# A short-sequence attention kernel: the output stores of 34 of 48 units on GpSimd's queue instead of 24, ten of them directly behind its last load

## Chip, cores, metric

One core of a Trainium2 chip. The time is the device time of one execution in microseconds (us), as a median of several executions. A "span" is the time from the first to the last instruction of a profiled execution, about 1.8 us less than that execution's time. Executions of this kernel scatter by about 1% on either side, so small differences are judged by the means of fast runs of the same rounds and their 95% intervals. A run is called slow when it lies more than 1.5% above the fastest of the same kernel, and fast otherwise. In profile lines POOL is GpSimd, SP is SyncE, ACT is ScalarE, DVE is VectorE and PE is TensorE; a q marks the sequencer of an engine, which issues its DMAs.

## The reference

```python
batch, n_heads, seq, head_dim = 32, 12, 128, 64        # q, k, v: f32
scores = (1.0 / np.sqrt(64)) * np.matmul(q, k.transpose(0, 1, 3, 2))
attn = np.exp(scores - scores.max(-1, keepdims=True))
attn = attn / (attn.sum(-1, keepdims=True) + 1e-8)
return np.matmul(attn, v)
```

There are 384 heads. The kernel works on **units** of 8 heads (48 units). q and k are loaded in 12 pieces of 4 units each, v in 12 groups of 4 units.

## The kernel before

GpSimd issues all loads (they cast f32 to bf16) and, among them, the stores of the first 24 units. SyncE issues the other 24, and not before unit `HELD` = 40 is normalised, so that its stores do not compete with the last loads. A store of two units goes out as two DMAs of 256 KB, so each unit costs one such DMA; I call that "a store" below.

```python
    stores = [1, 1] + [2] * ((NU - 4) // 2) + [1, 1]        # units per output buffer
    NQ, NVB, NVE, NP, NT, NA = 4, 2, 8, 4, 2, 4             # v: two buffers
    LAG, MIXED, HELD = 14, 24, NU - 8
    # ... one output buffer for each entry of stores, none is used twice
    mixed = [c for c in range(len(stores)) if sum(stores[:c + 1]) <= MIXED]

    def store(c):
        name = "POOL" if c in mixed else "SP"
        # ... emits one or two dma_start on that engine
        last = first + n - 1
        op(name, ("store", c), emit, [("N", last if c in mixed else max(last, HELD))])

    def act_keep(m):                                        # ScalarE: v out of PSUM
        # ... also waits for the landing of the v group that m + 1 begins
        op("ACT", ("K", m), lambda: keep_v(m), deps, ["act_pe"], v_landing(m + 1))

    # loads sorted by the step that needs them; a v load waits until the buffer
    # of two groups earlier is read
    todo = list(range(len(stores)))
    for _, kind, x in loads:
        pool_load(kind, x)
        while kind == "k" and todo[0] in mixed and sum(stores[:todo[0] + 1]) <= 4 * x - LAG:
            store(todo.pop(0))
    for c in todo:
        store(c)
```

The softmax here doesn't subtract the row's maximum and nothing guards it: scores larger than these inputs give would overflow.

## Time and profile before

| | before |
|---|---|
| time, median (3 runs) | 138.57 us |
| span of the profiled run | 135.7 us |
| busiest engine | TensorE, 70% |
| DMA moved | 37.75 MB read, 12.58 MB written |
| stores: GpSimd / SyncE | 24 / 24 |
| unit 40 normalised | 114.08 us |
| last unit normalised | 126.25 us |
| last store landed | 134.0 us |

The rows of 40 slices are read like this: each digit (in the GB/s row each number) is one slice of 3.4 us, and the digit is the busy share in tenths. The slices, the waits and the hole are shown in the prediction. Two lines of GpSimd's timeline (start, duration, engine, line, instruction; in brackets the idle time before it and what ended it):

```profile
95.92 0.73 POOL L400 DMA_DIRECT2D k_b<-in_k_dram  x1
103.43 0.74 POOL L388 DMA_DIRECT2D v_b<-in_v_dram  x1 [6.78 <-PE v_ps L187]
```

The second is GpSimd's last instruction in the kernel before: it has nothing to do for the last 32 us. "Landed" in this text is the time at which the sixteenth of a DMA's sixteen completion records came (one from each DMA engine); the first of them shows how far the quick DMA engines are. (The two DMAs of a store of two units count on one semaphore, so there only the first record of the first and the last of the second are sure.)

### The profile page before, as it was taken

The numbers are of one execution on the slowest core, as the hardware profiler recorded it, in microseconds if no ns is written. First come the engines' busy times: TensorE is split into PE (matmuls) and PEld (weight loads), VectorE is DVE, ScalarE is ACT, GpSimd is POOL, SyncE is SP. The second block draws the span as 40 slices with busy tenths as digits, with TensorE's granted clock in tenths as the row PEclk, the third lists the DMA queues.
The fourth block names the chain that finished last, engine by engine and source line by source line (L and its number), as shares of the span: only waits on it lengthen the run. The fifth ranks groups of instructions, "written<-read, shape, count | busy, mean of one in ns | idle before, by whom it ended". The sixth has DMA issues, their size and how long they took to land. (4 is left out here: it accounts for less than half of the span.)

```text
span 135.7 us, 6988 instructions
## 1 busy us (share of the span) xinstructions
PE 94.8 (70%) x3072; PEld 67.4 (50%) x3072; DVE 89.6 (66%) x204; ACT 73.8 (54%) x97; POOL 44.0 (32%) x65
## 2 busy tenths in 40 slices
PE   0055789899999786777499788599787979864000
PEld 0043367676667554555376556466555666542000
DVE  1155457999999699299079499288598798655200
ACT  0002548787885871862664754754855867793000
POOL 6920006064392935805900942801402000000000
PEclk9999999999999999999959999959999999999555
DMA  2999999999999999999999999999999960999993
GB/s 16 176 197 210 209 215 208 204 213 205 213 279 214 212 355 205 208 354 204 210 345 223 215 345 220 218 341 224 218 276 212 207 100 21 341 338 342 342 339 132
DMA packets 21320, 31.56 MB, mean 233 GB/s; under 512 B 1344, under 2 KB 13632, under 8 KB 21312
## 3 DMA queue, kind: packets, MB, share of 16 engines
q0 software_dynamic: 14784, 25.17, 89.9%
q1 hardware_dynamic: 6528, 6.29, 14.0%
q8 instruction: 4, 0.07, 0.2%
q14 instruction: 4, 0.03, 0.1%
HBM read 37.75 MB, written 12.58 MB: 371 GB/s over the span
## 5 line engine op out<-in xcount | busy, mean ns | idle before, releaser
L238 ACT ACTIVATE attnT<-s_ps 128x1024 bf16<-128x1024 f32 x48 | 49.4, 1030 | 0.3 <-PE s_ps L213 0.2
L233 ACT CAST v_e<-v_ps 128x512 bf16<-128x512 f32 x48 | 28.2, 588 | 36.6 <-PE v_ps L187 20.3
L173 PE MATMUL qk_ps<-ident,pair 128*128 128x128 bf16 x384 | 32.1, 231 | 15.2 <-PEq L466 14.9
L187 PE MATMUL v_ps<-v_b,sel 128*32 128x256 bf16 x768 | 31.5, 287 | 10.8 <-PEq L466 10.8
L256 DVE COPY qkT<-qk_ps 128x1024 bf16<-128x1024 bf16 x48 | 32.8, 683 | 5.7 <-PE qk_ps L173 4.6
L268 DVE TENSOR_TENSOR o_sb<-o_ps,recip 128x512 f32<-128x512 f32 x48 | 33.2, 691 | 1.7
L173 PEld LDWEIGHTS qk_ps<-ident,pair 128*128 128x128 bf16 x384 | 23.9, 103 | 19.7 <-issue 18.3
L388 POOL DMA_DIRECT2D v_b<-in_v_dram x12 | 9.2, 771 | 58.9 <-PE v_ps L187 54.3
L187 PEld LDWEIGHTS v_ps<-v_b,sel 128*32 128x32 bf16 x768 | 16.8, 98 | 17.2 <-issue 13.1
L225 PE MATMUL o_ps<-v_e,attnT 128*32 128x65 bf16 x1536 | 21.2, 197 | 3.9 <-PEq L466 3.5
L247 DVE COPY pair<-q_b 128x1024 bf16<-128x1024 bf16 x24 | 10.5, 437 | 19.1 <-DMA q_b<-in_q_dram 18.9
L225 PEld LDWEIGHTS o_ps<-v_e,attnT 128*32 128x32 bf16 x1536 | 15.7, 98 | 9.8 <-issue 6.3
L213 PE MATMUL s_ps<-qkT 64*128 64x128 bf16 x384 | 19.5, 222 | 0.6 <-PEq L466 0.5
L213 PEld LDWEIGHTS s_ps<-qkT 64*128 64x128 bf16 x384 | 11.1, 95 | 11.0 <-issue 11.0
L377 POOL DMA_DIRECT2D out_dram<-o_sb x22 | 15.9, 747 | 0.0
L265 DVE RECIPROCAL recip<-o_ps 128x8 f32<-128x8 f32 x48 | 9.7, 203 | 7.4 <-PE o_ps L225 6.6
L247 DVE COPY pair<-k_b 128x1024 bf16<-128x1024 bf16 x24 | 10.2, 426 | 0.0
L400 POOL DMA_DIRECT2D q_b<-in_q_dram x12 | 8.8, 732 | 1.0 <-SPq L93 1.0
L400 POOL DMA_DIRECT2D k_b<-in_k_dram x12 | 8.8, 735 | 0.0
L233 ACT ACT_TABLE_LOAD x1 | 1.3, 1283 | 12.8 <-DMA v_b<-in_v_dram 12.8
L545 DVE COPY sel<-ident 128x128 bf16<-128x128 bf16 x2 | 0.4, 223 | 1.7 <-POOL ident L520 1.7
L374 POOL DMA_DIRECT2D out_dram<-o_sb x2 | 1.5, 753 | 0.0
(8 smaller groups left out, 1.4 us busy)
## 6 DMA issues: line engine op xcount, KB each, us to landing
q_b<-in_q_dram POOLq DMA_DIRECT2D x12, 512.0 KB, 12.1
k_b<-in_k_dram POOLq DMA_DIRECT2D x12, 512.0 KB, 13.9
v_b<-in_v_dram POOLq DMA_DIRECT2D x12, 512.0 KB, 10.2
out_dram<-o_sb POOLq DMA_DIRECT2D x24, 256.0 KB, 14.4
out_dram<-o_sb SPq DMA_DIRECT2D x24, 256.0 KB, 3.3
```

The lines of the kernel that those rows point to most:

```text
L173: i = nc.tensor.transpose(p[:, :, r4, jj, :], x[:, r].rearrange("p a d -> p (a d)"), ident[:])
L187: x = nc.tensor.matmul(t[r4 * 32:(r4 + 1) * 32, i, :, :], lhsT=pick[:, w * nh + i, jv, :], rhs=v_b[g % NVB][:, :n, (4 * jv + r4) * D:(4 * ...
L213: i = nc.tensor.matmul(t[:, a, h, :], lhsT=x[p, 1, 4 * w + h, :], rhs=x[p, 0, 4 * w + h, :], start=True, stop=True)
L225: y = nc.tensor.matmul(t[h * SO:(h + 1) * SO, a, r * (D + 1):(r + 1) * (D + 1)], lhsT=x[:, a, h, r * SO:(r + 1) * SO], rhs=v_e[m % NVE][:, ...
L233: return nc.scalar.copy(v_e[m % NVE][:, :, :D], v_ps[:].rearrange("p (n e) -> p n e", e=D))
L238: return nc.scalar.activation(out=attnT[u % NA][:].rearrange("p a h (r s j) -> p (a h r) s j", r=4, j=J), in_=s_ps[u % 2][:].rearrange("p ...
L247: return nc.vector.tensor_copy(pair[t_index[t] % NP][:], src[:, 8 * b:8 * b + 8])
L256: return nc.vector.tensor_copy(x.rearrange("p h (r j s) -> p (h r) j s", r=4, j=J)[:, :, 2 * b:2 * b + 2, :].rearrange("p x j s -> p x (j ...
L265: nc.vector.reciprocal(r[:], o4[:, :, :, D]).then_inc(s_r, 1)
L268: return nc.vector.tensor_mul(o[:, :, w, :].rearrange("p a (r d) -> p a r d", d=D), o4[:, :, :, :D], r[:].unsqueeze(3).to_broadcast([128, ...
L377: e.dma_start(out=dst[:, a], in_=src[:, a]).then_inc(s_o[lane(c)], 16)
L400: nc.gpsimd.dma_start(out=bufs[x % NQ][:], in_=rows[R][:, n:n + 2, :]).then_inc(sm[x % NQ], 16)
```

## The change

The intent is to give the DMA engines something to do between the last load and unit 40: ten units' stores are queued on GpSimd directly behind its last load. The 24 stores among the loads are also spread more evenly, which puts them later.

```diff
-    LAG, MIXED, HELD = 14, 24, NU - 8
+    MIXED, OWN, HELD = 24, 34, NU - 8
-    mixed = [c for c in range(len(stores)) if sum(stores[:c + 1]) <= MIXED]
+    own = [c for c in range(len(stores)) if sum(stores[:c + 1]) <= OWN]
-        return c % 4 + (4 if c in mixed else 0)
+        return c % 4 + (4 if c in own else 0)
-        name = "POOL" if c in mixed else "SP"
+        name = "POOL" if c in own else "SP"
-        op(name, ("store", c), emit, [("N", last if c in mixed else max(last, HELD))])
+        op(name, ("store", c), emit, [("N", last if c in own else max(last, HELD))])
-        while kind == "k" and todo[0] in mixed and sum(stores[:todo[0] + 1]) <= 4 * x - LAG:
+        while kind == "k" and sum(stores[:todo[0] + 1]) <= MIXED * (x - 4) / (len(supers) - 5):
             store(todo.pop(0))
```

## The prediction

> **What bounds the kernel now.** I read the page's slices first, then its queues, then the sync engine's waits, and then narrow windows round the one hole in the slices.
>
> The page's rows of 40 slices (3.4 us each), its queues and its DMA issues:
> ```profile
> DMA  2999999999999999999999999999999960999993
> GB/s 16 176 197 210 209 215 208 204 213 205 213 279 214 212 355 205 208 354 204 210 345 223 215 345 220 218 341 224 218 276 212 207 100 21 341 338 342 342 339 132
> ...
> q0 software_dynamic: 14784, 25.17, 89.9%
> q1 hardware_dynamic: 6528, 6.29, 14.0%
> ...
> out_dram<-o_sb POOLq DMA_DIRECT2D x24, 256.0 KB, 14.4
> out_dram<-o_sb SPq DMA_DIRECT2D x24, 256.0 KB, 3.3
> ```
> The DMA engines are full from the second slice on, except for one hole two slices wide, some 20 us before the end. No compute engine is above 70%. So the time is roughly the DMA work, plus the start, plus the hole, plus the end. Before the hole GpSimd's queue runs (loads and 24 units' stores), after it SyncE's (the other 24 units' stores, 341 GB/s). GB/s counts written bytes; loads are cast from f32 to bf16, so 210 GB/s of loads is about 420 read.
>
> Why SyncE starts late (waits of SP), and the hole in half microseconds (the two last columns are the DMA share and GB/s):
> ```profile
> SPq L377 <- DVEq L477: 113.3, 1, 113.3
> ...
> 108.50:109.00 0.50, 0.11 (x12) 0.05 (x2) 0.50 (x2) 0.50 (x1) 0.00 (x0) 1.00 1.20 201
> ...
> 109.50:110.00 0.50, 0.50 (x18) 0.34 (x16) 0.50 (x1) 0.00 (x0) 0.00 (x0) 1.00 0.80 125
> 110.00:110.50 0.50, 0.50 (x28) 0.33 (x24) 0.30 (x2) 0.31 (x1) 0.00 (x0) 1.00 0.46 74
> 110.50:111.00 0.50, 0.33 (x32) 0.20 (x28) 0.50 (x2) 0.50 (x2) 0.00 (x0) 1.00 0.38 63
> 111.00:111.50 0.50, 0.35 (x7) 0.39 (x8) 0.47 (x3) 0.50 (x1) 0.00 (x0) 1.00 0.21 33
> 111.50:112.00 0.50, 0.50 (x17) 0.39 (x18) 0.50 (x1) 0.20 (x1) 0.00 (x0) 1.00 0.00 0
> ...
> 115.00:115.50 0.50, 0.45 (x8) 0.46 (x8) 0.47 (x2) 0.50 (x1) 0.00 (x0) 1.00 0.79 254
> ```
> The last load, v of group 11, ends here: the quick DMA engines finish at 109.5, the slow ones 2 us later. SyncE waits for unit 40's normalisation (13.39 + 0.69 after 100: done at 114.08) and its first bytes move after 115. Against a full share of about 1.12, the stretch 109.5 to 115.1 (5.6 us) did about 0.8 us of work: **4.7 us lost**. Meanwhile the output of units 24 to 39 lay ready, one unit every 2 us.
>
> The end (DVE and SP in the timeline):
> ```profile
> 125.56 0.69 DVE L268 TENSOR_TENSOR o_sb<-o_ps,recip 128x512 f32<-128x512 f32 x1
> 130.02 1.51 SPq L374 DMA_DIRECT2D out_dram<-o_sb  x2
> ```
> The last unit is done at 126.25, but SyncE, working off its 24 stores, issues its last one at 130.8. So today the store queue sets the end, 4.5 us behind the compute. By the trace's completion records that store has landed at 134.0; the span ends at 135.67, 1.67 us later.
>
> **What the Trainium skill says.** (1) "DMA: Bandwidth & Descriptors", section "Issuing engines are not separate DMA queues": all DMAs end on the same 16 engines, and another issuer only saves issue time. The trace agrees, with 342 GB/s of stores in SP's tail at a share above 1, so moving ten stores to GpSimd is worth only what it puts into the hole. (2) Same page, "Queues, rings and completion order": an engine goes round the queues that have work. Two queues in the tail thus share, and neither leaves engines idle; no trace here shows the two side by side. (3) Same page, "SWDGE vs HWDGE vs iDMA": a software-queue packet has up to 4096 B. The counts agree: SyncE's 6528 packets over 24 stores are 272 each (256 of 1 KB, 16 for completion), while q0's 14784 less my count of 12864 for the loads leaves 80 per store (64 of 4 KB and 16). (4) Same page, "Latency and other measured facts": some engines lag on the software path. The trace's lag was 1.1 us early and is 2.2 us from 60 us on (v of group 11: first completion 109.6, sixteenth 111.8).
>
> **The change part by part.** The completion records give each transfer's price. Without stores between, a q, k, v trio lands every 7.55 us (v at 12.7, 20.3, 27.9). With four stores per trio it is 10.0 (v at 75.4 and 85.4), so a GpSimd store between loads costs (10.0 - 7.55) / 4 = **0.62 us**. SyncE's 24 landed from 116.4 to 134.0: 17.6 / 23 = **0.765 us** each.
>
> (a) The 24 stores among the loads. I walked both loops by hand. Units stored ahead of v of group 4, 5, ... 11 are 2, 6, 10, 14, 18, 22, 24, 24 before; they become 0, 2, 6, 10, 12, 16, 20, 24. So all loads up to k of group 11 land 1 to 4 us earlier (q and k of group 11 by 4 x 0.62 = 2.5 us: 104.2 and 106.7 for 106.7 and 109.2), but **the last v stays behind all 24 stores**, at 111.8, if the queue never runs dry. I expect that it doesn't. Where stores are fewest, v of group 4 is issued at 36.05 while k of group 4 lands at about 40; later issues have 5 to 12 us ahead of them. The buffer waits of GpSimd (54.3 us for v) are slack and stay.
>
> (b) Compute. ScalarE's copy of the 44th v unit carries the wait for the last v. Before, it ran at 112.35, just after the landing. With compute 2.5 us ahead it is ready at 109.85 and waits until 111.85. So compute ends 0.5 us earlier, at about **125.75**: most of the lead is lost at that wait. Unit 40's output needs only earlier v's and comes at about 111.5 to 112.
>
> (c) GpSimd's ten last stores. They follow its last load (issued by 104.2 at the latest), 10 x 0.735 = 7.4 us of issuing, so until 111.6 at most; unit 33 was done by 99.5. They lie in the queues before the last v has ended, and each DMA engine goes straight on. The hole closes: -4.7 us. They cost ten times 0.62 to 0.765.
>
> (d) SyncE's 14 stores. From 112 to 114 it issues 6 ready ones in 4.4 us, then two per finished pair, and the last at 125.8. They cost 14 x 0.765 = 10.7 us.
>
> **The sum.** On the slowest DMA engine: 111.8 + (6.2 to 7.65) + 10.7 = 128.7 to 130.2. On the compute side: 125.8 for the last issue, plus 2.3 (SyncE's first store into empty queues, 114.15 to 116.4) to 3.3 (its median) = 128.1 to 129.1. The later decides: I take 129.4, plus 1.67, span 131.1 against 135.67: **4.6 us less**. 138.57 - 4.6 = **134.0 us**, 3.3% faster.
>
> **The rivals.** *Compute becomes the end.* The DMA and compute sums lie within a microsecond, so any delay of compute now counts, which it did not before (4.5 us of slack). The clock row speaks for it: TensorE was throttled to half for 3.4 us at 67.6 and 88.0, and again from 125.6. Were that third throttle to fall into 112 to 125, matmuls of some 2 us a unit would stretch by about 1.5 us: 135.5. DVE copies also took 0.64 rather than 0.43 us while GpSimd wrote a descriptor (at 103.76), but that is in the stretch where compute waits for v anyway. *The loads suffer.* Fewer early stores only help if DMA stays full; an idle microsecond near 36 to 44 us would push the last v back by as much. Against it stands the backlog above. Two microseconds lost there would give 136, "same". *The tail gets cheaper too.* Ten stores move from 1 KB packets at 0.765 to 4 KB ones at 0.62: another 1.4 us, which I counted only half. If the slow engines also catch up, the compute sum alone stays: span 130, time 132.8. *SyncE, starting some 2 us earlier, delays the last v.* At most one store's share, 0.7 us.
>
> **Range and chances.** 134.0; most of the gain is a hole that is visible and has data ready to fill it, so a loss is nearly excluded. The good rival gives 132.8, the throttle 135.5. Range 132.5 to 135.7. Faster by over 2% means below 135.8: 0.90. Same 0.09, slower 0.01.
>
> **What would show it.** Right: no slice below 9 in the DMA row between the second and the last two; GpSimd 34 stores and SyncE 14; a wait of ScalarE of about 2 us for the last v; the last v landing at 111 to 112.5; SyncE's first issue near 112; compute's end at 125 to 126.3; the last store issued within 1 us of the last normalisation, so that the chain that ended last reaches back into compute. Wrong: a dip of the DMA row early on, the last v later than 113, the last normalisation later than 127, or a hole still left between the last load and GpSimd's ten stores.

## The result

The time is 133.92 us (median of 4 runs, 132.37 to 135.5) against 138.74 for the kernel before in the same rounds. The ratio is 0.961, 95% interval 0.950 to 0.973. A ratio is the mean time of one kernel's fast runs over that of the other's of the same rounds, so it is not quite the ratio of the medians. The output is correct.

| | before | predicted | after |
|---|---|---|---|
| time, us | 138.57 | 134.0 | 133.92 |
| span, us | 135.7 | 131.1 | 130.6 |
| last v landed | 111.8 | 111.8 | 112.3 |
| last unit normalised | 126.25 | 125.75 | 125.97 |
| last store landed | 134.0 | 129.4 | 128.9 |

The page of the changed kernel, its slices and queues:

```profile
DMA  1999999999999999999999999999999999999991
GB/s 13 169 196 209 213 204 208 206 211 200 204 212 173 210 274 222 212 347 228 210 337 239 209 280 216 213 353 221 211 349 226 211 339 269 399 392 372 342 317 50
...
q0 software_dynamic: 15584, 27.79, 98.7%
q1 hardware_dynamic: 3808, 3.67, 8.2%
```

The hole is gone. The queues give the packet count of the prediction: ten more stores at 80 packets make 14784 + 800 = 15584, and 14 stores at 272 make 3808.

GpSimd's and SyncE's timelines in the changed kernel:

```profile
100.15 0.76 POOL L389 DMA_DIRECT2D v_b<-in_v_dram  x1 [4.69 <-PE v_ps L188]
100.90 7.08 POOL L378 DMA_DIRECT2D out_dram<-o_sb  x10
...
112.49 11.85 SPq L378 DMA_DIRECT2D out_dram<-o_sb  x12
124.47 1.95 SPq L375 DMA_DIRECT2D out_dram<-o_sb  x2
```

All ten stores are queued at 108.0, before the last v has ended on any DMA engine. What the DMA engines do then, in the same half microseconds as in the prediction (last two columns: DMA share, GB/s):

```profile
109.50:110.00 0.50, 0.50 (x12) 0.40 (x14) 0.47 (x3) 0.42 (x1) 0.00 (x0) 1.00 1.20 215
110.00:110.50 0.50, 0.50 (x18) 0.28 (x20) 0.42 (x1) 0.00 (x0) 0.00 (x0) 1.00 1.22 270
110.50:111.00 0.50, 0.50 (x36) 0.40 (x36) 0.45 (x1) 0.00 (x0) 0.00 (x0) 1.00 1.21 358
111.00:111.50 0.50, 0.35 (x35) 0.25 (x19) 0.50 (x3) 0.00 (x0) 0.00 (x0) 1.00 1.01 361
111.50:112.00 0.50, 0.50 (x8) 0.32 (x6) 0.47 (x3) 0.00 (x0) 0.00 (x0) 1.00 1.08 399
```

The GB/s climb while the slow DMA engines still finish v: each quick one goes over to stores at once. Before, the same lines fell from 125 to 0.

ScalarE's timeline of the changed kernel:

```profile
112.42 0.59 ACT L234 CAST v_e<-v_ps 128x512 bf16<-128x512 f32 x1 [2.50 <-DMA v_b<-in_v_dram]
```

Loads and compute run earlier than before (k of the last piece landed at 107.2 instead of 109.2), but the last v does not, and ScalarE waits 2.5 us for it. The end, from SyncE's waits (total, times, longest), and then the last line of DVE's timeline:

```profile
SPq L378 <- DVEq L478: 111.7, 1, 111.7
...
SPq L375 <- DVEq L478: 0.9, 1, 0.9
```

```profile
125.28 0.69 DVE L269 TENSOR_TENSOR o_sb<-o_ps,recip 128x512 f32<-128x512 f32 x1
```

The second wait is new. SyncE has caught up with compute: it waits 0.9 us for the last unit (125.97), where before it was 4.5 us behind.

### The profile page after: what moved, and what is told of

Its sections match the earlier page's. It is cut to its first block, busy times and chain, and to the rows that moved or that the text cites. A ratio compares the mean times of both kernels' runs of the same rounds, so it can differ in the third digit from the quotient of the medians.

```text
span 130.6 us, 6988 instructions
## 1 busy us (share of the span) xinstructions
PE 93.7 (72%) x3072; PEld 66.7 (51%) x3072; DVE 89.9 (69%) x204; ACT 73.5 (56%) x97; POOL 51.1 (39%) x75
## 3 DMA queue, kind: packets, MB, share of 16 engines
q0 software_dynamic: 15584, 27.79, 98.7%
## 5 line engine op out<-in xcount | busy, mean ns | idle before, releaser
L174 PE MATMUL qk_ps<-ident,pair 128*128 128x128 bf16 x384 | 31.5, 229 | 14.8 <-PEq L467 14.6
L174 PEld LDWEIGHTS qk_ps<-ident,pair 128*128 128x128 bf16 x384 | 23.4, 102 | 19.3 <-issue 17.9
L378 POOL DMA_DIRECT2D out_dram<-o_sb x32 | 23.0, 737 | 0.0
L375 POOL DMA_DIRECT2D out_dram<-o_sb x2 | 1.5, 753 | 0.0
```

Of the source, the lines that this page charges most:

```text
L174: i = nc.tensor.transpose(p[:, :, r4, jj, :], x[:, r].rearrange("p a d -> p (a d)"), ident[:])
L378: e.dma_start(out=dst[:, a], in_=src[:, a]).then_inc(s_o[lane(c)], 16)
```

## Experiments

My theory: the gain is the hole of 4.7 us, closed because stores lie queued behind the last load. Rivals: the even spread earns it by letting loads and compute run earlier; the issuer or its larger packets earn it; closing the hole in any way does. Then a second question: what sets the end now? Twelve kernels ran in three batches, each batch on one chip with its own runs of the kernel before, and each is timed over six runs. Times in "less than before" are differences of the means of fast runs. The profiled runs of skip6, mixed20, mixed20_own46, hold10 and early16 were slow ones. All intervals lie below 1; by a margin of 2%, however, spread_only, sp_after_v, sp_from_36 and hold10 count as unclear.

| run | ratio to before | 95% interval |
|---|---|---|
| ten_behind_only | 0.966 | 0.958 to 0.974 |
| spread_only | 0.986 | 0.978 to 0.993 |
| sp_after_v | 0.984 | 0.977 to 0.991 |
| sp_from_36 | 0.975 | 0.964 to 0.985 |
| skip6 (output wrong) | 0.944 | 0.937 to 0.950 |
| mixed20 | 0.953 | 0.947 to 0.960 |
| own40 | 0.960 | 0.955 to 0.965 |
| mixed20_own46 | 0.965 | 0.958 to 0.971 |
| after_again (the change itself) | 0.957 | 0.950 to 0.963 |
| hold10 | 0.983 | 0.976 to 0.991 |
| early20 | 0.963 | 0.954 to 0.972 |
| early16 | 0.967 | 0.961 to 0.973 |

### One half of the change alone

```diff
# ten_behind_only, against the changed kernel: the old places among the loads
-  ... <= MIXED * (x - 4) / (len(supers) - 5):
+  ... <= min(MIXED, 4 * x - 14):
# spread_only, against the changed kernel: no store behind the loads on GpSimd
-    MIXED, OWN, HELD = 24, 34, NU - 8
+    MIXED, OWN, HELD = 24, 24, NU - 8
```

> The ten stores go to GpSimd behind its last load, but the 24 stores among the loads keep the old places. Theory (the gain is the hole between the last load and SyncE's first store, filled by stores already queued): nearly the whole gain, profiled span 130.5 to 131.5 against 135.7; last v landing at about 112, ScalarE waits for it under 1 us instead of 2.5, last normalisation ends at about 126.2, DMA row without a hole. Rival (the even spread lets loads and compute run earlier and that earns a good part): a span of 133 or more.

> Only the even spread; the last 24 units stay with SyncE from unit 40 on. Theory: the last v still lands behind 24 stores at about 112, unit 40 is done near 112.4 instead of 114.1, so the hole shrinks by about 1.7 us and the span falls by that: about 134.0 (time ratio to before about 0.988). Compute ends near 126.0 as in the full change. Rival (spread earns most): a span under 132.5. Second rival (spread earns nothing): a span of 135.7.

**ten_behind_only** takes 4.7 us off (138.11 to 133.37), span 131.5, last v at 112.4, last normalisation 127.1 (126.2 expected). The full change's first ratio (0.961) lies inside its interval. So the ten queued stores earn nearly everything. That the gain is also the size of the hole is in part luck: in the profiled run compute set the end. SyncE waited for each of the last two units and issued the last store at 127.19:

```profile
SPq L375 <- DVEq L478: 2.0, 2, 1.2
```

Filling the hole could thus show only about as much as SyncE was behind compute before (4.5 us). What the spread adds is seen at the end of compute, 127.1 here against 125.97 and 126.67 in the two profiled runs of the full change.

**spread_only** takes 2.6 us off (2.0 by its ratio), more than the 1.7 I expected, span 133.3. Compute ended at 127.2 rather than 126.0; the clock was halved from 114.4 to 117.9 us in that run. Its windows of one microsecond:

```profile
109.00:110.00 1.00, 1.00 (x29) 0.68 (x28) 0.83 (x3) 0.35 (x1) 0.00 (x0) 1.00 1.22 214
110.00:111.00 1.00, 0.90 (x46) 0.70 (x42) 1.00 (x3) 0.00 (x0) 0.00 (x0) 1.00 0.68 111
111.00:112.00 1.00, 0.31 (x6) 0.13 (x3) 0.83 (x3) 0.00 (x0) 0.00 (x0) 1.00 0.14 23
112.00:113.00 1.00, 0.00 (x0) 0.00 (x0) 0.56 (x1) 0.32 (x1) 0.00 (x0) 1.00 0.25 83
113.00:114.00 1.00, 0.59 (x18) 0.41 (x20) 0.00 (x0) 1.00 (x2) 0.00 (x0) 1.00 1.04 340
```

The hole is 2.0 us (three microseconds that did 1.07 / 1.12 us of work), 2.7 less than before, and the time follows. The even spread brings unit 40 to 111.73 and so SyncE's start forward. It gains through the same hole, so the two halves (4.7 and 2.6) should not add up to the whole (5.4, and 6.1 when it was repeated): with ten stores in the hole, the spread has little left to shorten. The times point that way, but the ratios (3.4% and 1.4% against 3.9% and 4.3%) do not show it clear of noise.

### The hole closed by SyncE, or opened again

```diff
# sp_after_v, against the kernel before
-    LAG, MIXED, HELD = 14, 24, NU - 8
+    LAG, MIXED, HELD = 14, 24, 0
+            nc.sync.wait_ge(s_v[11 % NVB], 16 * (11 // NVB + 1))    # the last v has landed
             for o in program["SP"]:
# sp_from_36, against the kernel before
-    LAG, MIXED, HELD = 14, 24, NU - 8
+    LAG, MIXED, HELD = 14, 24, NU - 12
# hold10, against the changed kernel: the ten wait for unit 40 too
-  [("N", last if c in own else max(last, HELD))]
+  [("N", last if last < MIXED else max(last, HELD))]
```

> The kernel before, with SyncE waiting for the last v's landing instead of unit 40: the same 24 stores on the same queue, started as early as possible without running beside a load. Theory: start at about 112.0 instead of 114.15, so 2.1 us less: span about 133.6. What is left to the full change (130.6), about 3 us, is the idle of the quick DMA engines from 109.6 on, the start of the queue (about 1 us), and ten stores at SyncE's 0.765 instead of about 0.65 us (1.1 us). Rival (the issuer doesn't matter, only that SyncE starts late): a span of 131.

> The kernel before, with SyncE held to unit 36 instead of 40: it starts about 8 us earlier, at about 105.2, with 36 of the last units' stores competing with the last loads. Theory (the store queue shares the DMA engines with the loads, so the DMA hole closes but the last k and v are pushed back by what the stores take, 2 to 5 us, and compute then ends the kernel): last v landing at 114 to 117, last normalisation 128 to 131, span 132 to 135. Rival (closing the hole in any way is enough): last v at 112, span 130.5 to 131.

> The full change, but GpSimd's ten stores behind its loads also wait for unit 40. Same issuers, same packets, same places among the loads; only the hole is opened again. Unit 40 is done near 112 in the full change, while the quick DMA engines end the last v at 109.9. Theory (what counts is that stores lie queued when the last load ends): a dip in the DMA row, about 2 us more than the full change in the same batch, span 132.2 to 133.5, a ratio of about 0.98. Rival (what counts is who issues, or the cheaper packets): as the full change. Against the earlier run that had the same times but SyncE for these ten (span 133.3), the ten cheaper stores should give 1.1 us.

**sp_after_v** takes 2.1 us off, the size expected. Its profiled run shows half of it: the last v landed at 113.0, so SyncE started 1.1 us earlier than before and the span was 134.6, 1.1 less (133.7 to 134.6 over the fast runs). Waiting for a landing on another engine did not close the hole: the quick DMA engines are idle from about 110, and the first bytes moved 0.9 us after the issue at 113.04.

**sp_from_36** takes 3.8 us off, span 131.9 in the profiled run, 133.8 in one of its three fast ones. There is no hole between loads and stores in its DMA row. But its stores compete with the loads: the last v landed at 114.2 and compute ended at 128.05, 2 us later than in the full change. This is the theory's direction, at the mild end of the range I gave. It is also a partial point for the rival: closing the hole with SyncE's stores gets most of the gain, and its interval reaches down to 0.964, so the times alone do not tell it from the full change (0.950 to 0.973).

**hold10** is the sharpest of the three: same issuers, same packets, same places among the loads, only the ten stores 13 us later. It gives back 3.8 us of the change's 6.1 in that batch (136.54 against 132.78). Its windows, and GpSimd's timeline (the profiled run was slow, so only the pattern is read from it):

```profile
111.00:112.00 1.00, 1.00 (x29) 0.66 (x26) 0.86 (x2) 0.27 (x1) 0.00 (x0) 1.00 0.89 155
112.00:113.00 1.00, 0.89 (x45) 0.71 (x40) 0.96 (x4) 0.00 (x0) 0.00 (x0) 1.00 0.35 57
113.00:114.00 1.00, 0.23 (x5) 0.06 (x1) 0.86 (x2) 0.00 (x0) 0.00 (x1) 1.00 0.11 17
114.00:115.00 1.00, 0.00 (x0) 0.00 (x0) 0.48 (x1) 0.56 (x2) 1.00 (x2) 1.00 0.32 103
115.00:116.00 1.00, 0.83 (x24) 0.59 (x24) 0.00 (x0) 1.00 (x3) 1.00 (x2) 1.00 1.00 324
```

```profile
114.00 7.10 POOL L378 DMA_DIRECT2D out_dram<-o_sb  x10 [12.20 <-DVEq L478]
```

The hole is back, about 2.5 us of it. The loss is larger than my 2 us; that the stores after the hole are also dearer (324 GB/s here, 340 in spread_only's fast run, about 400 without a hole) is a likely reason, not a shown one. And the second half of the expectation did not show: hold10 is no faster than spread_only (0.983 and 0.986, intervals overlapping), though it has ten stores of GpSimd's in the place of SyncE's. The 1.1 us that I expected of them would be 0.8%, which these intervals do not exclude. Ten stores on GpSimd instead of SyncE saved nothing that could be seen, which agrees with the Trainium skill, "DMA: Bandwidth & Descriptors", section "Issuing engines are not separate DMA queues".

### What sets the end after the change

```diff
# skip6, against the changed kernel: units 34 to 39 are not stored (and not waited for)
     for c in todo:
-        store(c)
+        if not 34 < sum(stores[:c + 1]) <= 40:
+            store(c)
# mixed20 / own40 / mixed20_own46, against the changed kernel
-    MIXED, OWN, HELD = 24, 34, NU - 8
+    MIXED, OWN, HELD = 20, 34, NU - 8     # mixed20
+    MIXED, OWN, HELD = 24, 40, NU - 8     # own40
+    MIXED, OWN, HELD = 20, 46, NU - 8     # mixed20_own46 (and no final wait on unused semaphores)
# early20 / early16: ten_behind_only with
+    MIXED, OWN, HELD = 20, 34, NU - 8     # early20
+    MIXED, OWN, HELD = 16, 34, NU - 8     # early16
# after_again: the changed kernel as it is
```

> The full change with SyncE's first six stores (units 34 to 39) left out, so the output is wrong there on purpose. It asks what sets the end after the change. If compute (last unit done at 125.97, its store issued at once, landed at 128.9): 2.3 us for a store into empty queues and 1.7 to the end, a span of 129.9 to 130.6, at most 0.7 us under the change's 130.6. If the store traffic: six stores at about 0.7 us less, a span of 126 to 127.

> The full change with 20 units' stores among the loads and 14 behind them instead of 24 and 10. The last v then lands about 2.5 us earlier (109.8), and compute ends at about 123.5. If compute alone set the end, the span falls to about 128. Theory (compute and store traffic end within a microsecond of each other, and the bytes are unchanged): the traffic takes over, last landing stays near 128.5 to 128.9, a span of 130.0 to 130.6, with SyncE's last issue no longer waiting for the last normalisation.

> The full change with GpSimd taking 16 units behind its loads and SyncE only the last 8. Six stores move from SyncE's 0.765 to about 0.65 us: 0.7 us less traffic. Theory (compute sets the end): a span of 129.9 to 130.6, as skip6. Rival (GpSimd's issue of 0.71 us a store and its waits for units 34 to 39 delay the traffic): a span above 131.

> Both limits moved at once: 20 units' stores among the loads, 26 behind them by GpSimd, SyncE only the last two. Compute ends near 123.5 as in mixed20, and 12 more stores cost 0.65 instead of 0.765 us (1.4 us less traffic). Theory: the last landing moves to about 127.5 to 128, a span of 129.0 to 129.8, some 1 us under the full change. If GpSimd's waits for each pair's normalisation or its slower issue bind, 130.5 or more.

> The full change unaltered, as the yardstick for the other three on this chip: a ratio to before of 0.957 to 0.968, span 130.5 to 132.

> The old early places for the stores among the loads, cut off at 20 units, so 14 behind the loads by GpSimd, SyncE the last 14. The DMA queue is kept full early (the even spread left 0.5 us idle at 36 to 44 us) and the last v lands about 2.5 us earlier than in the full change, at 109 to 110. Theory (traffic and compute end together; once compute is 2.5 us earlier, traffic alone sets the end): span 129.5 to 130.5, at most 1 us under the full change in its batch. If compute were the only limit: 128.

> The same with 16 units among the loads and 18 behind. The last v lands about 5 us earlier than in the full change, 107 to 108, compute ends at 121 to 123. Theory: traffic alone sets the end, so as early20 within 0.5 us. If compute were still the limit in early20, another 1 to 2 us less.

**skip6**: fast spans of 129.0 to 129.9, against 130.5 to 132.3 for after_again. Six stores at 0.7 us are 4.2 us of traffic, and a good part of it does not show: compute is a limit close by. But somewhat more than the 0.7 us I allowed was saved (1.3 points of ratio, about 1.8 us, from another batch, intervals just touching). That suggests that in most runs traffic is the later of the two by a microsecond or so; across two batches it is not shown.

**after_again** repeats the change: 0.957, span 130.7. In its profiled run the last unit was done at 126.67 and its store landed at 129.0, 2.3 us later, which is the time of a store into empty queues. In that run compute set the end; in the first profiled run (125.97 and 128.9) 0.6 us of queue came on top.

**own40** (0.960) and the full change (0.957, 0.961) cannot be told apart. Its profiled span of 130.5 was as expected, but it is its shortest: the other five fast runs took 131.1 to 132.3, where I had put the rival (GpSimd's issue and waits delay the traffic). The times do not decide between the two.

**mixed20** has the lowest ratio of the correct kernels, 0.953, but its interval and after_again's overlap widely, and they were not run in one batch. Whether it is better stays open. As far as its profiled run tells, a slow one, it did not do what it was meant to: the last v landed at 111.9 instead of 109.8 and compute ended at 125.7 instead of 123.5.

**mixed20_own46** was expected a microsecond under the full change, and came out at 0.965, no better than it; there too the last v landed late, at 112.3 (a slow run). **early20** and **early16** did not gain either (0.963 and 0.967 against 0.957 in their own batch; early16's last v landed at 110.0 instead of 107 to 108, in a slow run). early20 did what it was meant to do with the loads: the last v landed at 110.5 and ScalarE no longer waited for it. Still compute ended at only 125.30, 0.7 us earlier rather than 2.5, and the stores far later. Its clock was halved from 122.9 us on, in the changed kernel from 125.6; how much of the shortfall is due to that no run shows. Its timelines of DVE and SyncE, and its windows of two microseconds (the third column from the end is the clock):

```profile
124.61 0.69 DVE L269 TENSOR_TENSOR o_sb<-o_ps,recip 128x512 f32<-128x512 f32 x1
...
126.04 1.51 SPq L375 DMA_DIRECT2D out_dram<-o_sb  x2
```

```profile
110.00:112.00 2.00, 1.80 (x67) 1.28 (x65) 1.83 (x5) 1.33 (x3) 2.00 (x4) 1.00 1.04 409
114.00:116.00 2.00, 1.82 (x64) 1.27 (x64) 1.49 (x3) 1.39 (x3) 0.00 (x0) 1.00 1.03 385
118.00:120.00 2.00, 1.37 (x62) 0.90 (x52) 1.25 (x3) 1.92 (x3) 0.00 (x0) 1.00 1.03 356
122.00:124.00 2.00, 0.87 (x57) 0.67 (x61) 0.90 (x2) 0.39 (x1) 0.00 (x0) 0.72 0.95 326
126.00:128.00 2.00, 0.00 (x0) 0.00 (x0) 0.00 (x0) 0.00 (x0) 0.00 (x0) 0.50 1.03 341
```

SyncE no longer waits for the last unit; its last store landed at 131.0, 5.7 us after compute. So with four stores fewer in front of the last v, traffic alone sets the end, as the theory had it. What it got wrong is the price: the stores moved out from among the loads became dearer. Behind the loads they start at 409 GB/s (0.64 us each, the price among loads) and fall within 12 us to 326 to 341 (about 0.78 us). In mixed20_own46, with GpSimd alone storing at first, the rate falls in the same way (399 GB/s at 112 to 114, 332 at 122 to 124; a slow run), and in own40, a fast one, from 408 at 112 to 114 to 383 at 116 to 118. In these runs fewer stores among the loads meant more DMA time in all. But it is no rule of the place or of the time since the last load. In sp_from_36 the last v landed at 114.2, and SyncE's stores kept their rate for ten microseconds after it (383 GB/s at 114 to 116, 379 at 122 to 124). Its page shows both that and the missing hole (slices of 3.3 us; the last fall is the wait for compute):

```profile
DMA  1999999999999999999999999999999999999872
GB/s 10 175 202 208 210 208 211 174 205 187 198 211 284 212 240 330 211 233 335 218 224 341 219 220 344 221 214 350 221 211 285 210 209 266 367 380 380 300 268 80
```

## Why the prediction was right

- **The bound.** DMA work plus one hole: right. Filling the hole alone gives 4.7 us (ten_behind_only), opening it again takes most back (hold10). That the time was met within 0.1 us is luck: the four runs lie between 132.4 and 135.5, and the median of the repeat was 132.6.
- **Step (a), the loads.** q and k of the last piece landed at 104.7 and 107.2 (104.2 and 106.7 predicted), the last v at 112.3 (111.8). The half microsecond was lost where the rival "the queue runs dry near 36 to 44" put it, at a quarter of the size that I gave it. There the rate in loads alone was 196 GB/s, where the loads before and after run at about 210: 8 us x (1 - 196/210) = 0.5 us. But the DMA share was 1.15 meanwhile, so the trace shows slow packets and no idle engines; that the queue ran dry is not shown.
- **Step (b), compute.** ScalarE waited 2.5 us for the last v (2.0), and compute ended at 125.97 (125.75). Right: the lead of the loads is lost at that wait.
- **Step (c), the ten stores.** Queued by 108.0, no hole, and 0.65 us each on the quick DMA engines. The sum was right. The reason that I hinted at for their price, GpSimd's 4 KB packets, found no support: own40, mixed20_own46 and hold10 show no gain from the issuer. SyncE's stores with their 1 KB packets were nearly as cheap in sp_from_36 (379 to 384 GB/s from 114 to 124 us, 0.69 us each). What makes a store cheap stays open.
- **Step (d), SyncE.** First issue at 112.49 (112), the last one right at the last normalisation. The two queues did not share the engines as I had read the skill: no data of SyncE's moved before 115.98, and its first store had its first completion record at 117.12, 4.6 us after the issue (2.0 into empty queues, before) and about two stores' time after the first record of GpSimd's last pair (115.79). I had not worked that out; the engines stayed full meanwhile (DMA share 1.02 to 1.06 from 114 to 120).
- **The sum.** 128.9 for the last landing, inside both 128.7 to 130.2 (traffic) and 128.1 to 129.1 (compute). That the two lie within a microsecond of each other is what the second group of runs shows.
- **The rivals.** The half clock did not fall into 112 to 125 (the clock row of the page has 9 in every slice from 72 to 124 us; it was halved at 125.6). Cheaper packets as a source of more gain: not seen in any run, though a microsecond is within the noise.

What stays open: whether traffic or compute sets the end in a given run (the two profiled runs of the change differ), and why store bandwidth falls from about 400 to about 335 GB/s in the 12 us after the loads in early20, but not in sp_from_36. No run separates a limit of HBM writes from others.

## What to carry to other kernels

Where DMA is full except for one hole, look for data that is ready during the hole and queue it behind the last load in the same queue, ahead of time; here a start signal on another engine came too late for the quick DMA engines and cost another microsecond of start. Then check what you have displaced: here the next limits (the last v's landing, compute's end, the price of stores behind the loads) lay close by, and every further shift of stores gained nothing that could be measured. Two halves of a change can shorten the same idle stretch, so try each alone before crediting either.

## What the Trainium skill lacked or had wrong

- "DMA: Bandwidth & Descriptors", section "Queues, rings and completion order": that an engine goes round its queues packet by packet does not mean that a store gets its turn soon. SyncE's first store, issued at 112.49 beside GpSimd's backlog, moved its first data at 115.98 and had its first completion record at 117.12 (4.6 us), against 2.0 us into empty queues. The page gives no time for this, and no run varied the backlog alone.
- No page gives the price of a store by what surrounds it: 0.62 us per 256 KB among the loads, 0.765 us in a tail of stores only, about 400 GB/s falling to about 335 within 12 us behind the loads in early20, and 379 to 383 GB/s held for 10 us in sp_from_36.
- Same page, "Latency and other measured facts": the page names two DMA engines as usually slower and gives no size. At the last load of the kernel before, the eighth of the sixteen completion records came 0.8 us after the first, the thirteenth 1.9 and the last 2.2 (2.4 in the changed kernel), so more than two engines lag. That cost time in the kernel before because nothing was queued behind the load.
